# Hybrid decoder layer: softmax scaling, mix residuals and sums of squares go from GpSimd to VectorE

## The chip, the cores and the metric

The kernel runs on one core of one Trainium2 chip. The metric is device time in microseconds (us); lower is better. The engines are named as in the profile: PE is TensorE (matmuls; PEld its weight loads), DVE is VectorE, ACT is ScalarE, POOL is GpSimd, SP is SyncE, which issues the DMAs. [...]

## The reference

One layer over 1024 tokens of width 1024, in float32:

```python
h = rms_norm(x, norm_mix_g)
q, k, v, u, gate = split(h @ w_in)             # 512, 128, 128, 512, 512 columns
q = rms_norm(q per head, q_norm_g); k = rms_norm(k per head, k_norm_g)
a = sliding_window_gqa(q, k, v, sinks, rel_bias)   # 8 query heads, 2 kv heads, window 128
c = conformer_conv(u, gate, ...)                   # GLU, causal depthwise conv, layer norm, silu
mix = concat([rms_norm(a, attn_out_g), rms_norm(c, conv_out_g)])
x = x + mix @ w_out
h = rms_norm(x, norm_mlp_g)
x = x + square(relu(h @ w_mlp_up)) @ w_mlp_down    # hidden 4096
```

Inside the attention, for each block of 128 queries against the 256 keys of the block before and its own:

```python
s = q k^T * scale + bias, masked
m = max(max(s), sink)
p = exp(s - m)
p = p / (sum(p) + exp(sink - m))
o = p v
```

## The kernel before, in words

Tokens lie on the free axis, in two halves of 512 (`h` = 0 and 1), and channels on the partitions, in tiles of 128x512. Each float32 operand of the large products is split in two rounded parts, `hi` and `lo`, and a product is three matmuls (`whi` by `hi`, `whi` by `lo`, `wlo` by `hi`): L198 to L200 in the projections, L837 to L839 in the MLP's first part. The splits of the weights are L167 (`whi`, ACT) and L168 (`wlo`, DVE).

After the input projection the work is a list of generators that a hand-written string interleaves (input projection, attention units, convolution groups, norms, output projection, MLP). A tile framework then sets the order on each engine by a simulated time line, with raised priorities for some of the steps, so that an edit in one place can move instructions on every engine. PSUM has two banks for `mm` (products), two for `sc` (scores and broadcasts), two for `tr` (transposes), one for `o` and one for `x`. A product can begin only when an `mm` bank has been read out.

The attention is 16 units (head pair `j`, block pair `bp`), each in three steps that lie two units apart:
- `attn_a`: score matmuls (L567) into two `sc` banks, scaling by ACT (L574), then bias and row maximum by DVE (L575).
- `attn_b`: exponentials with their row sums by ACT (L591), the reciprocal `rd` of the sum by DVE (L594), and the scaling of the 128x1024 tile `s` by `rd` on POOL (L596, L597, L599). For the first block pair the tile is smaller, and this takes two instructions.
- `attn_c`: transposes of `s` (L616), their evacuation to `pT` (L603, on ACT or DVE by a table), the products with `v` (L625) into the `o` bank, and their evacuation into `Q` (L603).

`norm_half` normalises one half of one group (attention or conv) over its 512 channels. ACT squares each of the four sources (L637), DVE adds the squares into `nacc` (L638), PE sums over the partitions with four small matmuls (L642), DVE and POOL make the power −1/2 (L209, L210), PE broadcasts it (L393), DVE scales the four tiles (L648), ACT rounds each to the `hi` part of `mix` (L658), and POOL subtracts for the `lo` part (L659).

`out_conv` forms the conv half of the output projection: 12 matmuls into one `mm` bank, and DVE adds `x` to it (L727, tiles `X`, `Xp`, `Xq`). `out` does the attention half: 12 matmuls, DVE adds (L738), ACT squares (L743), and POOL adds the squares into `rbc` (L744), from which `x1_norm` makes the scale of the MLP's norm. `xn` (L768) applies that norm, and L763 (ACT) and L764 (DVE) split its result `n` into `x1g` for the MLP. Between the norms and the projections of one half stand units, products or MLP pieces of the other, which PE does meanwhile.

POOL does nothing else but the powers and a few memsets. No DMA is issued from it.

Of the kernel before, what the change touches and what calls it, by code (L numbers as in the profile page):

```python
# [12 lines left out]
F32 = mybir.dt.float32  # L13
F32R = mybir.dt.float32r
AF = mybir.ActivationFunctionType
ALU = mybir.AluOpType
AX = mybir.AxisListType

P = 128
# [48 lines left out]
class Builder:  # L68
# [42 lines left out]
    def dma(self, out, in_):  # L111
        d = self.nc.sync.dma_start(out, in_)
        if self.pinned:
            self.tc.keep_in_program_order(d)
        return d.ins
# [90 lines left out]
    def rsqrt(self, out, in_, scale, cols):  # L206
        nc = self.nc
        t = self.small("rs", cols)
        nc.vector.tensor_scalar(t, in_, scale, EPS, ALU.mult, ALU.add)  # L209
        nc.gpsimd.tensor_tensor(out, t, self.mhalf[:, :cols], ALU.pow)  # L210
# [368 lines left out]
    def attn_b(self, u):  # L579
        nc = self.nc  # L580
        s, j, bp = u["s"], u["j"], u["bp"]
        ns = self.nsink[:, j].rearrange("p b g -> p (b g)")
        nm, es, den, rd = (self.small(x, 4) for x in ("nm", "es", "den", "rd"))
        nc.vector.scalar_tensor_tensor(nm, u["mx"], -1.0, ns, ALU.mult, ALU.min)
        nc.vector.tensor_tensor(es, nm, ns, ALU.subtract)
        for i in range(4):
            lo = P if bp == 0 and i < 2 else 0
            with ExitStack() as c:
                if self.exp_after is not None:
                    c.enter_context(self.tc.issue_after(self.exp_after))  # L590
                nc.scalar.activation(s[:, i, lo:], s[:, i, lo:], AF.Exp, bias=nm[:, i:i + 1], accum_out=den[:, i:i + 1])  # L591
        self.last_exp = nc.scalar.activation(es, es, AF.Exp).ins
        nc.vector.tensor_tensor(den, den, es, ALU.add)
        nc.vector.reciprocal(rd, den)  # L594
        if bp == 0:
            nc.gpsimd.tensor_tensor(s[:, 0:2, P:], s[:, 0:2, P:], rd[:, 0:2].unsqueeze(2).broadcast_to([P, 2, P]), ALU.mult)  # L596
            nc.gpsimd.tensor_tensor(s[:, 2:4, :], s[:, 2:4, :], rd[:, 2:4].unsqueeze(2).broadcast_to([P, 2, 256]), ALU.mult)  # L597
        else:
            nc.gpsimd.tensor_tensor(s, s, rd.unsqueeze(2).broadcast_to([P, 4, 256]), ALU.mult)  # L599

    def evac(self, e, dst, src):
        nc = self.nc
# [26 lines left out]
    def norm_half(self, h, srcs, goff, kc0):  # L629
        nc = self.nc  # L630
        acc = self.half("nacc")
        for j, s in enumerate(srcs):
            if j == 0:
                nc.scalar.square(acc, s)
            else:
                sq = self.half("sq")
                nc.scalar.square(sq, s)  # L637
                nc.vector.tensor_tensor(acc, acc, sq, ALU.add)  # L638
        yield True
        ps = self.psum(TAGS["ns"])  # L640
        for i in range(4):
            nc.tensor.matmul(ps[:, i:i + 1], acc[:, i * P:(i + 1) * P], self.ones[:, 0:1], start=True, stop=True)  # L642
        rc = self.small("rc", 4)
        self.rsqrt(rc, ps[:, 0:4], 1.0 / 512, 4)
        yield True
        rb = self.bcast_ps(rc, TAGS["nb"])
        for j, s in enumerate(srcs):
            nc.vector.scalar_tensor_tensor(s, s, self.pv[:, goff + j:goff + j + 1], rb, ALU.mult, ALU.mult)  # L648
            if kc0 == 0:
                mt = self.a4(F32R, "mix", (P, 2, HT))  # L650
            elif h == 0:
                mt = self.mp.tile([P, 2, HT], F32R, tag="hg", name=self.nm("mix"), bufs=4)
            else:
                if j % 2 == 0:
                    pair = self.sp.tile([P, 2, 2, HT], F32R, tag="tw", name=self.nm("mix"), bufs=2)
                mt = pair[:, j % 2]
            self.mix[kc0 + j, h] = (mt[:, 0, :], mt[:, 1, :])
            nc.scalar.copy(mt[:, 0, :], s)  # L658
            nc.gpsimd.tensor_tensor(mt[:, 1, :], s, mt[:, 0, :].bitcast(F32), ALU.subtract)  # L659
        yield True  # L660

    def norm_attn(self, h):
# [67 lines left out]
    def out(self, h):  # L730
        nc = self.nc
        acc = self.rbc[:, self.hs(h)]
        for m in range(KC):
            w = self.next_w()
            ps = self.psum("mm")
            self.mm3(ps, w, [self.mix[kc, h] for kc in range(4)])
            X = self.X[m, h]
            nc.vector.tensor_tensor(X, ps, X, ALU.add)  # L738
            if m == 0:
                nc.scalar.square(acc, X)  # L740
            else:
                sq = self.half("sq")
                nc.scalar.square(sq, X)  # L743
                nc.gpsimd.tensor_tensor(acc, acc, sq, ALU.add)  # L744
            if m == KC - 1:
                self.sumsq[h] = acc
            yield True
# [409 lines left out]
```

## Time and profile before

| what | value |
|---|---|
| time before, median of 3 runs | 1023.99 us (1022.13 to 1025.24) |
| profiled execution: its own time / its span | 1022.33 us / 1020.4 us |
| mean granted TensorE clock | 0.983 |
| PE busy | 996.5 us, 98% of the span |
| DVE busy | 668.7 us, 66% |
| ACT busy | 493.2 us, 48% |
| POOL busy | 104.1 us, 10%, 82 instructions |

The profiled execution is one of the program's runs, and its span lies 1.93 us under its own time. Busy shares are means over the whole span. The input projection, the attention with the convolution, the output projection and the MLP follow one another with some overlap; the attention units lie at about 190 to 340 us after the span's start, and from about 420 us on only the MLP is left. POOL is busy between about 130 and 415 us only.

### The profile page before, as it was taken

The numbers are of one execution on the slowest core, as the hardware profiler recorded it, in microseconds if no ns is written. First come the engines' busy times: TensorE is split into PE (matmuls) and PEld (weight loads), VectorE is DVE, ScalarE is ACT, GpSimd is POOL, SyncE is SP. The second block draws the span as 40 slices with busy tenths as digits, with TensorE's granted clock in tenths as the row PEclk, the third lists the DMA queues.
The fourth block names the chain that finished last, engine by engine and source line by source line (L and its number), as shares of the span: only waits on it lengthen the run. The fifth ranks groups of instructions, "written<-read, shape, count | busy, mean of one in ns | idle before, by whom it ended". The sixth has DMA issues, their size and how long they took to land.

```text
span 1020.4 us, 14870 instructions
## 1 busy us (share of the span) xinstructions
PE 996.5 (98%) x5560; PEld 806.2 (79%) x5560; DVE 668.7 (66%) x1150; ACT 493.2 (48%) x946; POOL 104.1 (10%) x82
## 2 busy tenths in 40 slices
PE   8999999899979989999999999999999999999998
PEld 7888887677657768778888888888888888888886
DVE  7456535266667484598777786777774777747763
ACT  7332325766757445475444544536454343443442
POOL 1000012255143322200000000000000000000000
PEclk9999999799979999999999999999999999999999
DMA  9123300002200234446556655667875532346451
GB/s 354 60 70 136 125 32 11 11 12 93 73 11 32 90 122 139 145 171 215 194 194 220 237 185 205 239 225 255 285 264 188 183 130 99 103 135 216 165 165 42
DMA packets 67464, 148.72 MB, mean 146 GB/s; under 512 B 7776, under 2 KB 8032, under 8 KB 66880
## 3 DMA queue, kind: packets, MB, share of 16 engines
q1 hardware_dynamic: 67248, 147.75, 42.3%
q8 instruction: 44, 0.72, 0.3%
q14 instruction: 28, 0.23, 0.1%
q10 hardware_dynamic: 144, 0.02, 0.0%
HBM read 106.98 MB, written 38.80 MB: 143 GB/s over the span
## 4 chain that ended last, share of the span: by engine, by line
PE 89%; DVE 5%; ACT 3%; issue 1%; DMA 1%; POOL 0%; DVEq 0%; SPq 0%; ACTq 0%
PE mm L198 7%; PE mm L199 7%; PE mm L200 7%; PE sc L837 4%; PE sc L839 4%; PE sc L838 4%; PE tr L839 3%; PE tr L837 3%; PE tr L838 3%; PE sc L567 3%; PE mm L839 3%; PE mm L837 3%; PE mm L838 3%; PE mm L1057 3%; PE mm L1058 3%; PE mm L1059 3%
## 5 line engine op out<-in xcount | busy, mean ns | idle before, releaser
L763 ACT CAST wb<-wd 128x512 fp32r<-128x512 f32 x80 | 49.8, 622 | 111.3 <-DVE wd L1025 41.7
L764 DVE TENSOR_TENSOR wb<-wd,wb 128x512 fp32r<-128x512 f32 x80 | 55.3, 691 | 69.9 <-ACT wb L763 69.9
L167 ACT CAST whi<-raw 128x512 fp32r<-128x512 f32 (+1 forms) x54 | 42.9, 795 | 77.2 <-PE mm L199 55.4
L198 PE MATMUL mm<-xh,whi 128*128 128x512 f32 x192 | 77.8, 405 | 0.0
L199 PE MATMUL mm<-xl,whi 128*128 128x512 f32 x192 | 77.2, 402 | 0.0
L200 PE MATMUL mm<-xh,wlo 128*128 128x512 f32 x192 | 77.2, 402 | 0.0
L764 DVE TENSOR_TENSOR wb<-hb,wb 128x512 fp32r<-128x512 f32 x112 | 76.8, 685 | 0.0
L837 PE MATMUL sc<-op,wb 128*128 128x512 f32 x192 | 74.7, 389 | 0.0
L838 PE MATMUL sc<-op,wb 128*128 128x512 f32 x192 | 74.7, 389 | 0.0
L839 PE MATMUL sc<-op,wb 128*128 128x512 f32 x192 | 74.7, 389 | 0.0
L763 ACT CAST wb<-hb 128x512 fp32r<-128x512 f32 x112 | 69.0, 616 | 0.3 <-PE sc L839 0.3
L168 DVE TENSOR_TENSOR wlo<-raw,whi 128x512 fp32r<-128x512 f32 (+1 forms) x54 | 52.8, 979 | 16.8 <-ACT whi L167 11.5
L763 ACT CAST wb<-raw 128x512 fp32r<-128x512 f32 x46 | 27.7, 621 | 65.4 <-DVE raw L891 33.0
L198 PE MATMUL mm<-mix,whi 128*128 128x512 f32 x128 | 52.6, 412 | 3.3 <-ACT x1g L763 2.9
L200 PE MATMUL mm<-mix,wlo 128*128 128x512 f32 x128 | 52.5, 410 | 0.3 <-DVE wlo L168 0.3
L199 PE MATMUL mm<-mix,whi 128*128 128x512 f32 x128 | 52.4, 410 | 0.0
L1058 PE MATMUL mm<-wb,wb 128*128 128x512 f32 x128 | 49.8, 389 | 0.0
L1058 PE MATMUL sc<-wb,wb 128*128 128x512 f32 x128 | 49.8, 389 | 0.0
L837 PE MATMUL tr<-op,wb 128*128 128x512 f32 x128 | 49.8, 389 | 0.0
L838 PE MATMUL tr<-op,wb 128*128 128x512 f32 x128 | 49.8, 389 | 0.0
L1059 PE MATMUL mm<-wb,wb 128*128 128x512 f32 x128 | 49.6, 389 | 0.0
L1059 PE MATMUL sc<-wb,wb 128*128 128x512 f32 x128 | 49.6, 389 | 0.0
(270 smaller groups left out, 2532.9 us busy)
## 6 DMA issues: line engine op xcount, KB each, us to landing
hb<-hid SPq DMA_DIRECT2D x112, 256.0 KB, 2.9
wd<-w_down SPq DMA_DIRECT2D x80, 256.0 KB, 4.4
raw<-w_up SPq DMA_DIRECT2D x27, 512.0 KB, 3.5
hid<-h SPq DMA_DIRECT2D x48, 256.0 KB, 2.9
pa<-pa SPq DMA_DIRECT2D x20, 512.0 KB, 4.5
raw<-w_out SPq DMA_DIRECT2D x32, 256.0 KB, 2.6
hid<-pa SPq DMA_DIRECT2D x32, 256.0 KB, 2.9
hid<-tu SPq DMA_DIRECT2D x32, 256.0 KB, 3.3
```

Of the source, the lines that this page charges most:

```text
L167: self.pin(nc.scalar.copy(hi, raw))
L168: self.pin(eng.tensor_tensor(lo, raw, hi.bitcast(F32), ALU.subtract))
L198: nc.tensor.matmul(ps, w[0][:, ws], xh, start=first, stop=False)
L199: nc.tensor.matmul(ps, w[0][:, ws], xl, start=False, stop=False)
L200: nc.tensor.matmul(ps, w[1][:, ws], xh, start=False, stop=last)
L763: self.pin(self.nc.scalar.copy(hi, src))
L764: self.pin(eng.tensor_tensor(lo, src, hi.bitcast(F32), ALU.subtract))
L837: nc.tensor.matmul(ps, wh[:, c], xh, start=first and k == 0, stop=False, skip_group_check=True)
L838: nc.tensor.matmul(ps, wh[:, c], xl, start=False, stop=False, skip_group_check=True)
L839: nc.tensor.matmul(ps, wl[:, c], xh, start=False, stop=last and k == len(xs) - 1, skip_group_check=True)
L1058: nc.tensor.matmul(pss[m], wh[:, c], bl, start=False, stop=False, skip_group_check=True)
L1059: nc.tensor.matmul(pss[m], wl[:, c], bh, start=False, stop=f == NP - 1, skip_group_check=True)
```

## The change

Three kinds of POOL instructions become DVE instructions; POOL keeps the powers (L210, L375, L507). The scaling of `s` was one instruction per unit (two for `bp` = 0), with `rd` broadcast over the row; it becomes four per unit, one for each row block, with `rd` as the scalar operand. That makes 56 of 128x256 and 8 of 128x128. The 16 subtractions of `mix` and the 14 additions into `rbc` only change their engine.

```diff
@@ attn_b
         nc.vector.reciprocal(rd, den)
-        if bp == 0:
-            nc.gpsimd.tensor_tensor(s[:, 0:2, P:], s[:, 0:2, P:], rd[:, 0:2].unsqueeze(2).broadcast_to([P, 2, P]), ALU.mult)
-            nc.gpsimd.tensor_tensor(s[:, 2:4, :], s[:, 2:4, :], rd[:, 2:4].unsqueeze(2).broadcast_to([P, 2, 256]), ALU.mult)
-        else:
-            nc.gpsimd.tensor_tensor(s, s, rd.unsqueeze(2).broadcast_to([P, 4, 256]), ALU.mult)
+        for i in range(4):
+            lo = P if bp == 0 and i < 2 else 0
+            nc.vector.tensor_scalar(s[:, i, lo:], s[:, i, lo:], rd[:, i:i + 1], None, ALU.mult)
@@ norm_half
             nc.scalar.copy(mt[:, 0, :], s)
-            nc.gpsimd.tensor_tensor(mt[:, 1, :], s, mt[:, 0, :].bitcast(F32), ALU.subtract)
+            nc.vector.tensor_tensor(mt[:, 1, :], s, mt[:, 0, :].bitcast(F32), ALU.subtract)
@@ out
                 nc.scalar.square(sq, X)
-                nc.gpsimd.tensor_tensor(acc, acc, sq, ALU.add)
+                nc.vector.tensor_tensor(acc, acc, sq, ALU.add)
```

Lines behind the first edit have a number lower by two in the changed kernel (L642 becomes L640, L648 L646, L727 L725), and the scaling is its L597.

The framework gives another order on the engines. Two places matter.

The first is PE around the sum over partitions of the first attention norm (L642 before, on `nacc_2748`; L640 after, on `nacc_2774`). Before, this stands in a row on PE, from the products with `v` (`o_2686`) that are the last to go into that sum to the broadcast of its power:

```order
L625 MATMUL o_2686<-pT_2687,v 64x128 x2
L567 MATMUL sc_2712<-kh,Q_501 128x256 x2
L625 MATMUL o_2686<-pT_2687,v 64x128 x6
L616 MATMUL tr_2811<-ident,s_2463 128x128 x4
L616 MATMUL tr_2879<-ident,s_2561 128x128 x4
L616 MATMUL tr_2885<-ident,s_2561 128x128 x4
L642 MATMUL o_2759<-ones,nacc_2748 128x1 x4
L625 MATMUL o_2803<-pT_2804,v 64x128 x8
L393 MATMUL sc_2768<-ident,rc_2764 128x128 x4
```

Now this does, where `o_2712` are the same products:

```order
L614 MATMUL tr_2834<-ident,s_2480 128x128
L623 MATMUL o_2712<-pT_2713,v 64x128 x8
L614 MATMUL tr_2834<-ident,s_2480 128x128 x3
L614 MATMUL tr_2840<-ident,s_2480 128x128 x4
L198 MATMUL mm_2759<-mix_1967,whi_2674 128x512
L199 MATMUL mm_2759<-mix_1967,whi_2674 128x512
L200 MATMUL mm_2759<-mix_1967,wlo_2675 128x512
L614 MATMUL tr_2911<-ident,s_2581 128x128 x4
L614 MATMUL tr_2917<-ident,s_2581 128x128 x4
L640 MATMUL o_2785<-ones,nacc_2774 128x1 x4
L623 MATMUL o_2832<-pT_2833,v 64x128 x8
L393 MATMUL sc_2794<-ident,rc_2790 128x128 x4
```

Matmuls of the conv half of the output projection (`mm_2759`) have moved in between; the 9 of `mm_2759` before these three, and the last 3 of `mm_2680`, stand directly ahead of the first row, where before the same matmuls (as `mm_2733` and `mm_2657`) all stood earlier, ahead of the scores and transposes that come before these rows.

The second is DVE around the scaling of the second attention norm (L648 before, L646 after), where the conv half of the output projection ends and the MLP's norm of the first half begins. Before, it does:

```order
L648 SCALAR_TENSOR_TENSOR Q_501<-Q_501,pv,sc_3383 128x512 x4
L768 SCALAR_TENSOR_TENSOR n_571_3404<-Xp_2329,pv,rbc 128x512
L768 SCALAR_TENSOR_TENSOR n_578_3431<-Xp_2329,pv,rbc 128x512
L727 TENSOR_TENSOR Xq_3339<-mm_3449,xr_3447 128x512
L168 TENSOR_TENSOR wlo_3475<-raw_3409,whi_3474 128x512
L727 TENSOR_TENSOR X_3493<-mm_3480,xr_3478 128x512
L768 SCALAR_TENSOR_TENSOR n_578_3431<-X_2598,pv,rbc 128x512
L168 TENSOR_TENSOR wlo_3506<-raw_3441,whi_3505 128x512
```

Now it does (`mm_3493`, `mm_3524` and `mm_3555` are the products that were `mm_3449`, `mm_3480` and `mm_3511`):

```order
L725 TENSOR_TENSOR Xq_3383<-mm_3493,xr_3491 128x512
L168 TENSOR_TENSOR wlo_3519<-raw_3453,whi_3518 128x512
L646 SCALAR_TENSOR_TENSOR Q_501<-Q_501,pv,sc_3427 128x512 x4
L725 TENSOR_TENSOR X_3537<-mm_3524,xr_3522 128x512
L657 TENSOR_TENSOR mix_3433<-Q_501,mix_3433 128x512
L168 TENSOR_TENSOR wlo_3550<-raw_3485,whi_3549 128x512
L657 TENSOR_TENSOR mix_3437<-Q_501,mix_3437 128x512
L657 TENSOR_TENSOR mix_3441<-Q_501,mix_3441 128x512
L657 TENSOR_TENSOR mix_3445<-Q_501,mix_3445 128x512
L766 SCALAR_TENSOR_TENSOR n_571_3448<-Xp_2341,pv,rbc 128x512
L766 SCALAR_TENSOR_TENSOR n_578_3475<-Xp_2341,pv,rbc 128x512
L766 SCALAR_TENSOR_TENSOR n_578_3475<-X_2618,pv,rbc 128x512
```

The evacuation of `mm_3493` has moved ahead of the four scalings, and the four subtractions L657, which were POOL's, stand with three `xn` ahead of the evacuation of `mm_3555`, which is the next row. Behind that row come a weight split, the evacuation of the following product (`mm_3582`), a weight split of 128x1024, the two `lo` parts `x1g_3450` and `x1g_3477`, three more `xn`, the evacuation of `mm_3605`, another weight split of 128x1024, and the `lo` part `x1g_3482`. On PE, 5 matmuls of `mm_3524` follow the broadcast `sc_3427`, then the 12 of `mm_3555`, the 12 of `mm_3582`, the 12 of `mm_3605`, and the MLP's `mm_3627` from `x1g_3450`, `x1g_3477`, `x1g_3482` and `x1g_3509`, three matmuls each.

## Rows read from the trace of the kernel before

**Rows 1.** The page: span, and busy time of each engine.

```profile
span 1020.4 us, 14870 instructions
PE 996.5 (98%) x5560; PEld 806.2 (79%) x5560; DVE 668.7 (66%) x1150; ACT 493.2 (48%) x946; POOL 104.1 (10%) x82
```

**Rows 2.** Windows: stretch, length, PE, PEld, DVE, ACT, POOL busy, PEclk, DMA share, GB/s.

```profile
320.00:350.00 30.00, 30.00 (x192) 22.41 (x193) 16.80 (x31) 18.70 (x44) 13.71 (x9) 1.00 0.19 62
350.00:380.00 30.00, 26.61 (x124) 21.45 (x123) 23.15 (x36) 12.11 (x21) 8.41 (x6) 0.94 0.38 124
600.00:700.00 100.00, 100.00 (x443) 82.77 (x442) 74.59 (x120) 46.47 (x82) 0.00 (x0) 1.00 0.66 231
```

**Rows 3.** Windows of two more stretches.

```profile
397.00:415.00 18.00, 18.00 (x81) 14.92 (x80) 9.00 (x12) 8.63 (x13) 9.72 (x7) 1.00 0.44 147
...
200.00:283.00 83.00, 83.00 (x460) 61.02 (x460) 51.99 (x149) 56.25 (x162) 34.54 (x23) 0.96 0.18 58
```

**Rows 4.** Windows around the two attention norms.

```profile
283.50:289.20 5.70, 1.46 (x13) 0.99 (x11) 3.42 (x13) 5.63 (x22) 1.89 (x1) 0.88 0.00 0
289.20:309.00 19.80, 18.43 (x77) 13.19 (x77) 11.37 (x25) 8.17 (x22) 10.13 (x7) 0.60 0.00 1
361.90:390.00 28.10, 24.71 (x101) 19.35 (x101) 23.23 (x32) 13.32 (x23) 6.41 (x4) 0.94 0.29 95
```

**Rows 5.** PE's time line, 280 to 298 us: start, us, instruction, [idle before].

```profile
286.59 0.66 PE L616 MATMUL tr<-ident,s 128*128 128x128 f32 x4 [2.29 <-ACT pT L603]
289.20 1.87 PE L642 MATMUL o<-ones,nacc 128*128 128x1 f32 x8 [1.95 <-DVE nacc L638]
```

**Rows 6.** POOL's time line, 276 to 302 us.

```profile
280.02 1.89 POOL L599 TENSOR_TENSOR s<-s,rd 128x1024 f32<-128x1024 f32 x1 [7.72 <-DVE rd L594]
286.70 1.89 POOL L599 TENSOR_TENSOR s<-s,rd 128x1024 f32<-128x1024 f32 x1 [4.79 <-DVE es L585]
```

**Rows 7.** DVE's time line, 276 to 288 us.

```profile
280.09 2.11 DVE L575 CUSTOM_DVE_ANT_0 s<-s,bias 128x256 f32<-128x256 f32 x1
...
285.74 0.43 DVE L575 CUSTOM_DVE_ANT_0 s<-s,bias 128x256 f32<-128x256 f32 x1
...
287.10 2.04 DVE L638 TENSOR_TENSOR nacc<-nacc,sq 128x512 f32<-128x512 f32 x1 [0.52 <-ACT sq L637]
```

**Rows 8.** The chain of waits, 276 to 300 us: start, us, what.

```profile
286.54 0.54 ACT sq L637
```

**Rows 9.** POOL's groups: count, busy us, mean ns, idle before and its releasers.

```profile
L599 POOL TENSOR_TENSOR s<-s,rd 128x1024 f32<-128x1024 f32 x12 | 23.8, 1980 | 49.2 <-DVE rd L594 17.8 <-ACT whi L167 9.9 <-PE o L625 8.9
L744 POOL TENSOR_TENSOR rbc<-rbc,sq 128x512 f32<-128x512 f32 x14 | 19.5, 1392 | 49.7 <-ACT sq L743 45.8 <-ACT es L592 4.0
...
L659 POOL TENSOR_TENSOR mix<-Q,mix 128x512 fp32r<-128x512 f32 x8 | 11.8, 1502 | 10.8 <-ACT mix L658 10.8
L659 POOL TENSOR_TENSOR mix<-y,mix 128x512 fp32r<-128x512 f32 x8 | 11.0, 1390 | 5.0 <-ACT mix L658 5.0
```

**Rows 10.** DVE's groups, shapes apart.

```profile
L764 DVE TENSOR_TENSOR wb<-hb,wb 128x512 fp32r<-128x512 f32 x112 | 76.8, 685 | 0.0
L575 DVE CUSTOM_DVE_ANT_0 s<-s,bias 128x256 f32<-128x256 f32 x56 | 37.8, 706 | 6.0 <-ACT s L574 5.8
...
L603 DVE COPY Q<-o 128x256 f32<-128x256 f32 x6 | 2.5, 424 | 5.1 <-PE o L625 5.1
...
L518 DVE COPY kc<-rk 128x512 f32<-128x512 f32 x2 | 0.8, 424 | 0.0
```

**Rows 11.** The time line of all engines, 361.9 to 369 us.

```profile
362.26 2.72 DVE L648 SCALAR_TENSOR_TENSOR Q<-Q,pv,sc 128x512 f32<-128x512 f32 x4 [2.99 <-PE sc L393]
...
364.90 2.42 DVE L768 SCALAR_TENSOR_TENSOR n<-Xp,pv,rbc 128x512 f32<-128x512 f32 x2
...
367.24 0.68 DVE L727 TENSOR_TENSOR Xq<-mm,xr 128x512 f32<-128x512 f32 x1
...
368.07 0.47 PE L198 MATMUL mm<-mix,whi 128*128 128x512 f32 x1 [2.87 <-ACT x1g L763]
```

## The prediction

> **What bounds the kernel now.** I read the page first. PE is busy for 996.5 of 1020.4 us [rows 1], so anything this change can win is time in which PE waits, or runs at the lower clock level. The windows say where that is. From 420 us on nothing that the change touches is left, and there PE is full: 100.00 busy of 100.00 us, clock 1.00, 443 matmuls, so 0.2257 us for one of 128x512 [rows 2]. From 200 to 283 us PE is full as well (83.00 of 83.00), although most of the units are scaled there and half of the `mix` subtractions done; so it is from 320 to 350 us [rows 2, 3]. PE waits in two places, each at an attention norm [rows 4]: 4.24 us from 283.5 to 289.2 and another 1.37 us up to 309, and 3.39 us from 361.9 to 390. Behind the first wait the granted clock falls: 0.60 on average over 19.80 us. With only the levels 1.0 and 0.5, that is the lower one for 80% of it, 15.8 us, which cost at most 7.9 us.
>
> The time lines then show why PE waits. At 286.59 it had waited 2.29 us for transposes, and at 289.20 1.95 us for the sum of squares `nacc` [rows 5]. Both go back to a DVE instruction that was slow beside a POOL one: the bias step begun at 280.09 took 2.11 us while POOL scaled `s` from 280.02 for 1.89; the same step at 285.74, beside no POOL work, took 0.43. The add into `nacc`, begun at 287.10, took 2.04 beside the next scaling (286.70, 1.89) [rows 6, 7], where an add of this shape has a mean of 0.685 [rows 10]. So in these places the two engines did not work side by side: the DVE instruction ended when POOL's did.
>
> The second place is another story. PE waited 2.87 us at 368.07; the row names an ACT split, but that matmul begins a new product, and what came free last for it is the `mm` bank, read out by the DVE add begun at 367.24. This add stood behind the four scalings of `Q` (362.26, 2.72 us) and two `xn` (364.90, 2.42 us) [rows 11].
>
> **The change part by part.** *What DVE takes on.* The nearest rows for a scaling of 128x256 are 0.43 (the bias step, two inputs and a maximum [rows 7]) from above and half of the 0.424 of a 128x512 copy between SBUF tiles, 0.21, from below; a 128x256 copy out of PSUM took 0.424 [rows 10]. I take 0.35, and 0.30 for the eight halves: 56 x 0.35 + 8 x 0.30 = 22.0 us. The 16 subtractions are the shape and kind of L764, 0.685 each, 11.0 us; the 14 adds likewise, 9.6 us. Together 42.6 us. What DVE gets back is the stretch under POOL: the 56 bias steps alone took 37.8 us and at 0.43 would take 24.1, so at least 13.7 us; at most what POOL spent in the four groups that go, 66.1 us [rows 9, 10]. I take 25, about twice the one group. DVE ends near 686 us, 67% of the span: not a bound as a whole, but each of its queues counts.
>
> *A. First attention norm, 283 to 309 us.* The chain that ends in `nacc` is now: evacuation of `o` 0.42 [rows 10], the square 0.54 [rows 8], the add 0.685, with gaps some 2 us. PE has in that time, by the new order, 15 transposes (four took 0.66 [rows 5], so 2.5 us if none overlap) and three matmuls of 0.23: 3.2 us. So the sum need not wait. The wait of 2.29 us for transposes falls for two reasons: the bias step is no longer stretched, which gives 1.68 us, and 12 matmuls (2.7 us) now stand ahead of them. I leave 0.7 us of the 4.24 for what is late next (the broadcast's chain through POOL's power, which stays): −3.5, bounds 0 and −4.24. The clock: it fell behind a gap of 5.70 us in which PE did 1.46 us of work [rows 4]. If that gap is filled, the fall may not come, −7.9; the rest of the norm's chain (sum, power, broadcast, scaling, split) is still there with little PE work beside it, so it may come as before, 0. No row tells which; I take less than half, −3.5. A = −7.0, bounds 0 and −12.1.
>
> [...]
>
> *B. Second attention norm, 362 to 390 us.* Now: 28.10 us for 101 matmuls, which at 0.2257 want 22.8, so 5.3 us lost: 3.39 of waiting and, at a clock of 0.94, 1.7 by the lower level [rows 2, 4]. After: the evacuation of `mm_3493` is moved ahead of the scalings, so the wait of 2.87 goes. Take its successor, `mm_3555`, in time from the broadcast `sc_3427`. DVE does four scalings (2.72), one add, four subtractions, a split and three `xn`, then the add that frees the bank: ten more of 0.62 (the mean in the full stretch, 74.59 us for 120 [rows 2]) to 0.685, so 8.9 to 9.6 us. PE has 5 + 12 + 12 matmuls until it needs that bank, 29 x 0.2257 = 6.5 us, and 0.3 to 0.5 us more as the split in that queue is late for it. It waits 2.0 to 2.5 us. Then the MLP's first product: its `lo` part `x1g_3482` is 11 DVE instructions further on, two of them of double length, so 13 x 0.62 to 0.685 = 8.1 to 8.9 us after the bank. PE has 12 + 7 matmuls for that time, 4.3 us, and loses 3.8 to 4.6 us, part of it already at the `hi` parts. With the 0.3 to 0.5 for the split and some 0.5 at the product after, 6.6 to 8.1 us are lost in place of 5.3, if the clock holds; one more spell at the lower level adds 1.7. I take 7.5: B = +2.2, bounds 0 (DVE faster than 0.62 with POOL silent) and +4.6.
>
> *C. The other units, and the `mix` subtractions of the convolution, 191 to 283 and 302 to 350 us.* PE is full there [rows 2, 3], which is what hides POOL's work now and DVE's then; DVE is busy 63% and 56% of it. 0; bounds −3.3 (clock 0.96 over 83 us, if it stayed up) and +2 (one more spell at the lower level).
>
> *D. The sums of squares, seven in 320 to 350 and seven in 397 to 415 us.* They end in a norm that is wanted much later. In 397 to 415 us PE is full and DVE half idle (9.00 of 18.00); seven adds of 0.685 fill 4.8 us of the 9.0 [rows 3]. 0; without that cover they would cost their 4.8 us.
>
> Sum: −7.0 + 2.2 = −4.8 us. The profiled execution goes from 1022.33 to 1017.5 us; it lies 1.66 us under the median of the runs, so for that 1023.99 − 4.8 = **1019.2 us**.
>
> **The rivals.** *Nothing to measure.* The first norm gains little (−2 to −3: the waits shrink, the clock falls all the same), and the second takes it back (+2.2): 1023 to 1024. For it speaks that PE was full in most of the stretch; against it that 4.24 us of waiting has its cause in the stretched instructions.
>
> *Both clock terms fall away:* A is −12.1 and B as above, −9.9: 1014. For it: the fall came behind a gap that should close.
>
> *Slower by DVE's queue at the second norm.* The bank of `mm_3555` comes free behind four subtractions that POOL had done beside DVE. If 8.1 us are lost, the clock falls once more (B = +4.6), and at the first norm only 1.4 us is won: +3.2, 1027.2. It decides itself where that bank comes free later than 6.5 us after the broadcast; by the order it does, so the question is the size.
>
> *Slower by small pieces.* One unit is now scaled in four instructions, 1.4 us of DVE's queue per unit where POOL's 1.98 stood beside it. If the evacuations and the splits of weights behind them come 0.7 us late (half of it) for PE in each of the 11 units between 200 and 302 us, that is +7.7, with −4.8 together +2.9: 1026.9. Against it: PE is full in 83.00 us of 83.00 with DVE at 51.99 even with all the stretch.
>
> [...]
>
> **How the numbers follow.** About 0.3%, 3.1 us, is what a measurement of this kernel can tell from no change. Forecast (A −5 to −9, B +1 to +3) 0.42; both clock terms gone 0.18; nothing to measure 0.20; DVE's queue 0.13; small pieces 0.07. So faster 0.60, same 0.20, slower 0.20. The forecast's own range is 1016 to 1022 us. For 8 in 10 the range goes down to 1010.5 (the best case with some of C's bound) and up to 1027.5 (the slower cases).
>
> **What would show it.** Right: POOL about 30 us; no bias step above 0.5 us except beside a power; no PE wait above 1 us between 283 and 290 us; a wait of about 2 us at the first matmul of `mm_3605` and of 3 us or more at a `lo` part of `x1g`; windows from 420 us on unchanged. A clock of 0.6 behind the first norm would take half of A away. Wrong: PE waits in 200 to 283 us, behind DVE's scalings or evacuations; or scalings of 0.5 us and more each, since B's and C's queues then are longer than I worked out.

## The result, and the profile after

The changed kernel takes 1011.66 us (median of 4 runs, 1009.68 to 1013.01), the one before 1023.12 us beside it: a ratio of 0.9882, with a 95% interval of 0.9864 to 0.9901, so 11.5 us less. It was forecast at 1019.2. The profiled execution went from a span of 1020.4 to 1010.1 us.

The page of the changed kernel, to be held against [rows 1]:

```profile
span 1010.1 us, 14850 instructions
...
PE 989.2 (98%) x5560; PEld 802.9 (79%) x5560; DVE 677.4 (67%) x1244; ACT 491.8 (49%) x946; POOL 30.9 (3%) x32
```

Its windows (columns as in [rows 2]); the stretches answer to those of [rows 2 to 4]:

```profile
200.00:283.00 83.00, 83.00 (x450) 62.19 (x451) 52.07 (x194) 58.01 (x171) 10.08 (x4) 0.95 0.15 50
283.50:289.20 5.70, 5.45 (x53) 4.42 (x50) 4.79 (x16) 4.40 (x14) 1.01 (x1) 1.00 0.30 94
289.20:309.00 19.80, 18.87 (x117) 13.34 (x118) 16.82 (x59) 14.26 (x41) 0.00 (x0) 1.00 0.04 14
...
350.00:380.00 30.00, 24.81 (x101) 18.43 (x100) 22.89 (x35) 13.13 (x22) 0.00 (x0) 0.94 0.27 90
...
600.00:700.00 100.00, 100.00 (x443) 82.84 (x442) 72.93 (x118) 47.60 (x83) 0.00 (x0) 1.00 0.67 233
```

At the first attention norm PE is now busy for 5.45 of 5.70 us where it was for 1.46, and in the 19.80 us behind it the clock is 1.00 where it was 0.60. The second norm still has its waits, and from 420 us on nothing moved.

DVE's groups, shapes apart:

```profile
L575 DVE CUSTOM_DVE_ANT_0 s<-s,bias 128x256 f32<-128x256 f32 x56 | 22.4, 420 | 5.1 <-ACT s L574 4.8
...
L597 DVE TENSOR_SCALAR s<-s,rd 128x256 f32<-128x256 f32 x56 | 16.2, 349 | 0.3
...
L742 DVE TENSOR_TENSOR rbc<-rbc,sq 128x512 f32<-128x512 f32 x14 | 9.7, 690 | 0.8
...
L657 DVE TENSOR_TENSOR mix<-Q,mix 128x512 fp32r<-128x512 f32 x8 | 5.2, 686 | 0.0
...
L597 DVE TENSOR_SCALAR s<-s,rd 128x128 f32<-128x128 f32 x8 | 1.9, 282 | 0.1
```

The bias step went from a mean of 706 ns [rows 10] to 420: no instruction stands beside a scaling on POOL any more. PE's time line at the first norm, where [rows 5] had two waits of about 2 us:

```profile
286.44 1.04 PE L640 MATMUL o<-ones,nacc 128*128 128x1 f32 x8
287.73 1.09 PE L623 MATMUL o<-pT,v 128*64 128x128 f32 x16 [0.26 <-DVE rs L209]
...
291.96 1.13 PE L567 MATMUL sc<-kh,Q 64*128 64x256 f32 x4 [0.93 <-ACT s L574]
```

And at the second norm, 340 to 395 us, the two longest waits:

```profile
360.58 0.47 PE L198 MATMUL mm<-mix,whi 128*128 128x512 f32 x1 [1.91 <-ACT x1g L761]
...
368.35 0.50 PE L836 MATMUL mm<-x1g,whi 128*128 128x512 f32 x1 [2.50 <-DVE x1g L762]
```

DVE's time line ahead of the first of them shows the queue that was forecast:

```profile
351.51 2.72 DVE L646 SCALAR_TENSOR_TENSOR Q<-Q,pv,sc 128x512 f32<-128x512 f32 x4 [1.20 <-PE sc L393]
354.15 0.68 DVE L725 TENSOR_TENSOR X<-mm,xr 128x512 f32<-128x512 f32 x1
354.75 0.68 DVE L657 TENSOR_TENSOR mix<-Q,mix 128x512 fp32r<-128x512 f32 x1
...
355.95 1.89 DVE L657 TENSOR_TENSOR mix<-Q,mix 128x512 fp32r<-128x512 f32 x3
357.76 1.41 DVE L766 SCALAR_TENSOR_TENSOR n<-Xp,pv,rbc 128x512 f32<-128x512 f32 x2
...
359.75 0.69 DVE L725 TENSOR_TENSOR X<-mm,xr 128x512 f32<-128x512 f32 x1
```

The add at 359.75 frees the bank, and PE's matmul at 360.58 is the one that needed it.

**A ledger.** Two numbers of each profile explain most of what sets its span apart from the others': PE's idle time (the span less PE's busy time) and what the lower clock level costs. In windows of 0.1 us of the kernel before, the granted clock is 1.00 or 0.50 in 10,190 of 10,200; sixteen matmuls of L625 took 1.10 us at 1.00 (begun at 270.44) and 1.98 at 0.50 (begun at 305.74). With these two levels, the cost is at most (1 − mean clock) x span. The clock has three digits, so this is good to about 0.5 us. Rows of kernels from the experiments below are put in already.

| kernel | span | PE busy | idle | clock | lost by clock | rest |
|---|---|---|---|---|---|---|
| before | 1020.4 | 996.5 | 23.9 | 0.983 | 17.3 | 979.2 |
| full change | 1010.1 | 989.2 | 20.9 | 0.990 | 10.1 | 979.1 |
| scaling alone | 1019.2 | 997.0 | 22.2 | 0.982 | 18.3 | 978.7 |
| residuals of the mix alone | 1016.1 | 995.0 | 21.1 | 0.985 | 15.2 | 979.8 |
| full change, POOL loaded | 1016.3 | 994.2 | 22.1 | 0.985 | 15.2 | 979.0 |
| before, empty work on PE | 1016.5 | 995.8 | 20.7 | 0.991 | 9.1 | 986.7 |
| full change, subtractions later | 1004.6 | 985.3 | 19.3 | 0.993 | 7.0 | 978.3 |

The rest of these is the same within 1.5 us but for the kernel that has work added on PE; the seven profiles that are not in the table come to 977.8 to 980.6. So of the change's 10.3 us, 3.0 are PE's waits and 7.2 the clock, as far as this sum tells them apart.

### The profile page after: what moved, and what is told of

It reads as the page before. It is cut to its first block, busy times and chain, and to the rows that moved or that the text cites. A ratio compares the mean times of both kernels' runs of the same rounds, so it can differ in the third digit from the quotient of the medians.

```text
span 1010.1 us, 14850 instructions
## 1 busy us (share of the span) xinstructions
PE 989.2 (98%) x5560; PEld 802.9 (79%) x5560; DVE 677.4 (67%) x1244; ACT 491.8 (49%) x946; POOL 30.9 (3%) x32
## 3 DMA queue, kind: packets, MB, share of 16 engines
q1 hardware_dynamic: 67248, 147.75, 42.6%
## 4 chain that ended last, share of the span: by engine, by line
PE 90%; DVE 5%; ACT 3%; DMA 1%; issue 1%; SPq 0%; POOL 0%; DVEq 0%; ACTq 0%
PE mm L198 7%; PE mm L199 7%; PE mm L200 7%; PE sc L837 4%; PE sc L835 4%; PE sc L836 4%; PE tr L837 3%; PE tr L835 3%; PE tr L836 3%; PE sc L567 3%; PE mm L1055 3%; PE mm L1056 3%; PE mm L1057 3%; PE sc L1057 3%; PE sc L1055 3%; PE sc L1056 3%
## 5 line engine op out<-in xcount | busy, mean ns | idle before, releaser
L168 DVE TENSOR_TENSOR wlo<-raw,whi 128x512 fp32r<-128x512 f32 (+1 forms) x54 | 48.6, 901 | 17.4 <-ACT whi L167 12.3
L198 PE MATMUL mm<-mix,whi 128*128 128x512 f32 x128 | 51.2, 401 | 1.9 <-ACT x1g L761 1.9
L199 PE MATMUL mm<-mix,whi 128*128 128x512 f32 x128 | 50.6, 396 | 0.0
```

Of the source, the lines that this page charges most:

```text
L168: self.pin(eng.tensor_tensor(lo, raw, hi.bitcast(F32), ALU.subtract))
L198: nc.tensor.matmul(ps, w[0][:, ws], xh, start=first, stop=False)
L199: nc.tensor.matmul(ps, w[0][:, ws], xl, start=False, stop=False)
```

## The experiments

All ratios are to the kernel before, run beside on the same chip, with their 95% interval.

**One part at a time.** Three kernels each take one part of the diff:

```diff
 e1:  for i in range(4): nc.vector.tensor_scalar(s[:, i, lo:], ...)       # scaling only
 e2:  nc.vector.tensor_tensor(mt[:, 1, :], s, mt[:, 0, :] ..., subtract)   # residuals of the mix only
 e3:  nc.vector.tensor_tensor(acc, acc, sq, ALU.add)                       # sums of squares only
```

The scaling alone:

> Only the softmax scaling goes to VectorE; the residuals of the mix and the sums of squares stay on GpSimd. Theory P (the gain is the stretched VectorE work at the first attention norm, which the scalings on GpSimd cause): nearly the whole gain of the first norm is here, 8 to 11 us, and the second norm costs no more than before, since the four subtractions are still on GpSimd: 1011 to 1015 us, at or a little below the full change. Theory Q (all three parts add up, each by freeing its own stretched time): 3 to 6 us less than before, 1017 to 1020 us.

1020.78 us, 0.996 (0.994 to 0.998): theory P's time fell. The windows of this kernel say why:

```profile
225.00:250.00 25.00, 25.00 (x105) 17.88 (x102) 12.70 (x47) 14.77 (x44) 5.48 (x4) 0.65 0.06 22
...
283.00:309.00 26.00, 24.77 (x162) 17.62 (x162) 20.49 (x58) 16.89 (x49) 6.54 (x5) 1.00 0.20 62
```

The first norm was won, with 1.2 us of waiting and a clock of 1.00. But from 225 to 250 us, at the second convolution norm, the clock is 0.65, where before and after it is 0.93, and that takes most of the gain back. PE shows no idle time there. Its order at that place has changed: scores, the small sums, transposes and the broadcast follow one another with only a few large matmuls between. So what theory P said of the first norm holds, and the loss lies elsewhere.

The residuals alone:

> Only the 16 residuals of the mix go to VectorE. TensorE's order is that of before, row for row. Theory P: the first norm's waits of 2.29 and 1.95 us stay (the scalings still stand beside the bias step and the add), and the second norm gets the longer VectorE queue: 0 to +4 us against before. Theory Q: 2 to 4 us less than before.

1019.06 us, 0.9947 (0.9927 to 0.9967): 5.0 us less, a little beyond theory Q's figure and against P's. PE's order is that of before, but the scalings on POOL now fall at other moments. PE's time line, 270 to 312 us, and the windows at the norm:

```profile
284.91 0.66 PE L616 MATMUL tr<-ident,s 128*128 128x128 f32 x4 [0.70 <-ACT pT L603]
...
287.02 1.05 PE L642 MATMUL o<-ones,nacc 128*128 128x1 f32 x8 [1.45 <-DVE nacc L638]
```

```profile
283.50:289.20 5.70, 3.29 (x35) 2.71 (x33) 3.93 (x16) 3.50 (x12) 0.92 (x2) 1.00 0.30 92
289.20:309.00 19.80, 19.80 (x77) 13.49 (x73) 10.74 (x32) 9.64 (x27) 2.01 (x2) 0.66 0.00 1
```

The two waits of [rows 5] shrank from 4.24 to 2.15 us, since the add into `nacc` is no longer the instruction that is caught (0.68 us at 286.28 for 2.04). But the clock behind is 0.66, hardly above the 0.60 of before: with half of the wait gone, most of the spell at the lower level stays.

The sums alone:

> Only the 14 additions of squares go to VectorE. TensorE's order is that of before. Both theories of the stages say 0 (-1 to +1 us): TensorE is full where they lie. If GpSimd work anywhere costs time, -2 to -4 us.

1023.8 us, 1.0001 (0.9984 to 1.0017): nothing, as forecast. Their counterpart is the full change without them:

> The full change with the 14 sums of squares back on GpSimd. TensorE's order is that of the full change but for 9 rows. The sums alone did nothing, so the time should be that of the full change, 1010.5 to 1013 us; if the sums matter once the rest is gone, 1013 to 1016 us.

1012.85 us, 0.989 (0.9876 to 0.9905): the full change's time.

**Which residuals the scaling lacks.** The scaling and the convolution's residuals only:

```diff
+ (nc.vector if kc0 else nc.gpsimd).tensor_tensor(mt[:, 1, :], s, mt[:, 0, :]..., subtract)   # on e1
```

> The scaling and the eight residuals of the convolution's mix on VectorE; the eight of the attention and the sums of squares stay on GpSimd. The scaling alone had won the first attention norm, but lost most of it again to a spell of 20.5 us at the lower level from 232.5 us on, at the second convolution norm, where its order has few large matmuls; in this kernel the order at that place is that of the full change. Theory R (the convolution's residuals on GpSimd push that place into the bad order): the spell there is 3.4 us as in the full change, and the time 1010 to 1014 us. If the attention's residuals or the sums are what the scaling lacked: 1018 to 1021 us as with the scaling alone.

1009.63 us, 0.9862 (0.9843 to 0.9881): theory R by the time, just under its range. Its window at the second convolution norm:

```profile
225.00:250.00 25.00, 25.00 (x132) 18.59 (x130) 15.04 (x51) 15.85 (x44) 3.91 (x2) 0.86 0.19 53
```

The clock is 0.86 here, against 0.65 with the scaling alone. But the spell is about 7 us long, not the 3.4 that theory R named: the full change has 0.93, with PE's order at that place the same. So that order is not all that sets the spell. These two parts are the whole gain of the change; the sums and the attention's residuals add nothing to it.

**Order or stretch.** The full change moves instructions and frees DVE from POOL at once. This kernel keeps the order of the full change and loads POOL again:

```diff
+ for i in range(3):
+     nc.gpsimd.tensor_tensor(scr, scr, rd[:, i:i + 1].broadcast_to([P, 256]), ALU.mult)
```

> The full change, and behind each reciprocal three two-input GpSimd instructions of 128x256 on a tile that nothing else uses (0.66 us each by the rows of before, 32 us in all and some). The orders of VectorE and ScalarE are those of the full change, TensorE's too but for 8 rows. Theory S (stretch: work on GpSimd that reads SBUF holds VectorE up): bias steps of 2 us come back, VectorE's busy time grows by 10 to 25 us, and time grows by 2 to 8 us: 1014 to 1020 us. Theory O (the new order, with matmuls of the output projection at the first norm, is what won the time): no more than 1.5 us over the full change, 1011 to 1013.5 us, even with stretched instructions.

1016.7 us, 0.9925 (0.9907 to 0.9942): some 5 us over the full change, in theory S's range, but 6.8 us are still won against before. Its sign was another one, though: the bias steps stayed at 416 ns on average, and the scalings were stretched. A unit on DVE's and on POOL's time line:

```profile
273.78 2.36 DVE L599 TENSOR_SCALAR s<-s,rd 128x256 f32<-128x256 f32 x4
```

```profile
273.88 2.10 POOL L601 TENSOR_TENSOR scr<-scr,rd 128x256 f32<-128x256 f32 x3 [5.07 <-DVE rd L596]
```

DVE's group and the windows at the first norm:

```profile
L599 DVE TENSOR_SCALAR s<-s,rd 128x256 f32<-128x256 f32 x56 | 32.6, 638 | 0.3
```

```profile
283.50:289.20 5.70, 3.91 (x35) 2.70 (x33) 4.58 (x16) 3.42 (x12) 1.64 (x2) 1.00 0.30 92
289.20:309.00 19.80, 18.87 (x72) 13.12 (x73) 13.66 (x40) 10.44 (x33) 2.16 (x4) 0.66 0.05 14
```

The four scalings, beside POOL's three, now take 638 ns each for 349, and DVE's busy time grew by 17 us. On PE, whose order at the norm is that of the full change, two waits are new:

```profile
285.55 0.66 PE L618 MATMUL tr<-ident,s 128*128 128x128 f32 x4 [0.99 <-DVE pT L605]
...
289.16 1.64 PE L395 MATMUL sc<-ident,rc 128*128 128x128 f32 x8 [0.53 <-POOL rc L210]
```

With them the clock behind the norm is 0.66 again. So the stretch brings the lower level back even in the new order, and the full change needed the freed DVE. What the new order is worth by itself is not shown: no run has the old order with DVE freed.

The control with instructions on POOL that read nothing:

> Control of the run before: the same places, but GpSimd only sets the tile (8 instructions of 128x256 that read nothing, about 2 us in all per unit). If any GpSimd work holds VectorE up, the same 2 to 8 us over the full change; if it takes GpSimd instructions that read SBUF, bias steps stay at 0.42 us and the time within 1 us of the full change.

1014.12 us, 0.9893 (0.987 to 0.9916). It settles nothing: nothing held the memsets to the reciprocals, and they ran from 3 to 56 us, far from the attention. With a release that holds them there:

```diff
+ nc.vector.tensor_copy(scr[:, 0:1], rd[:, 0:1])
+ for _ in range(7):                             # behind the scalings
+     nc.gpsimd.memset(scr, 0.0)
```

> The control again, since in the first one the memsets ran from 3 to 56 us, far from the attention: a VectorE copy of one column behind each reciprocal now releases seven GpSimd memsets of 128x256 (0.31 us each by the first control, 2.2 us per unit), so that they lie beside the scalings. The order changes in about 100 of VectorE's 1200 rows, so the time tells little (1009 to 1019 us). The durations tell: if GpSimd work that reads nothing holds VectorE up too, scalings of 0.6 us and more as with the two-input load (638 ns on average there); if it takes reading, 350 ns as in the full change.

1018.1 us, 0.9948 (0.9924 to 0.9973), with another order, so that the time alone tells nothing of the memsets. DVE's time line, and POOL's beside it:

```profile
270.03 1.53 DVE L600 TENSOR_SCALAR s<-s,rd 128x256 f32<-128x256 f32 x4
271.49 0.67 DVE L168 TENSOR_TENSOR wlo<-raw,whi 128x512 fp32r<-128x512 f32 x1
272.08 0.41 DVE L577 CUSTOM_DVE_ANT_0 s<-s,bias 128x256 f32<-128x256 f32 x1
```

```profile
270.18 2.75 POOL L602 MEMSET scr<- 128x256 f32 x7 [3.16 <-DVE scr L597]
```

Neither of the two answers: the scalings are held a little (four in 1.53 us against 1.14 in the full change, 423 ns on average against 349), while the split and the bias step behind them, beside the same memsets, take 0.67 and 0.41 us, as in the first control with no memset beside them (0.68 and 0.42).

**Clock or waits.** The kernel before, with empty work for PE at the first norm:

```diff
+ with self.tc.issue_after(self.last_po):         # the last products with v
+     for _ in range(10):
+         nc.tensor.matmul(fl, m[:, :P], m, start=True, stop=True)
+ for _ in range(2):
+     nc.tensor.matmul(fl, self.ident, sq, start=True, stop=True)
```

> The kernel before with empty work on TensorE in the two gaps at the first attention norm: 10 matmuls of 128x512 after the last products with v, and 2 float32 matmuls on the last square ahead of the sum; their bank is never read. Up to that place the orders are those of before, and the stretched instructions on VectorE stay. Theory C (the clock fell because TensorE did little in those gaps): the two spells of 6.83 and 10.24 us at the lower level go, 8.5 us less: 1014 to 1017 us, although no wait of another engine is shorter. If the clock falls from what follows the norm (power, broadcast), or if it is the waits themselves that cost: within 2 us of before, 1021 to 1025 us.

1019.12 us, 0.9953 (0.9938 to 0.9968). PE's time line, and the window behind:

```profile
283.74 2.12 PE L643 MATMUL x<-mix 128*128 128x512 f32 x8
...
287.31 1.98 PE L645 MATMUL x<-sq,ident 128*128 128x512 f32 x4
289.82 1.02 PE L649 MATMUL o<-ones,nacc 128*128 128x1 f32 x8 [0.53 <-DVE nacc L638]
```

```profile
289.20:309.00 19.80, 18.83 (x123) 13.18 (x123) 15.01 (x39) 11.07 (x35) 10.48 (x7) 1.00 0.00 1
```

Theory C is right on the mechanism: with POOL's scalings still there, work that is thrown away kept the clock at 1.00 for these 19.8 us, and the kernel was faster by it. It missed on the size: 4 us in place of 8.5. By the ledger 8.2 us came back from the clock and 3.2 from the waits, but the rest is 7.5 us larger; the empty work is 4 to 4.5 of that, and the other 3 are open (the order behind the norm differs).

**One large scaling or four small.**

```diff
- for i in range(4): nc.vector.tensor_scalar(s[:, i, lo:], ...)
+ nc.vector.tensor_tensor(s, s, rd.unsqueeze(2).broadcast_to([P, 4, 256]), ALU.mult)
```

> The full change, but each unit is scaled by one VectorE instruction (128x1024, rd broadcast over the row; two for the first block pair) in place of four small ones. Rival of the small pieces: one large instruction takes less of VectorE's time than four at 0.35 us each and wins 2 us or more: 1007 to 1010 us. If the small pieces cost nothing, within 2 us of the full change, 1010 to 1013 us; it is a two-input form, so that one may take as long as 1.1 to 1.3 us, no less than the four.

1014.25 us, 0.9905 (0.9884 to 0.9925), not faster than the full change:

```profile
L599 DVE TENSOR_TENSOR s<-s,rd 128x1024 f32<-128x1024 f32 x12 | 14.7, 1222 | 0.2
```

One takes 1.22 us; four small ones follow one another at 16.2 / 56 = 0.29 us, 1.16 in all.

**The second norm.** The four subtractions of that norm are taken out of DVE's queue, first behind the first add of the MLP, then behind the last `x1g`:

```diff
- nc.vector.tensor_tensor(mt[:, 1, :], s, mt[:, 0, :]..., subtract)       # for kc0 == 0, h == 1
+ with self.tc.issue_after(self.pa_ins):     # e4; e8: self.x1_ins, the last residual of x1g
+     for mt, s in self.late: nc.vector.tensor_tensor(mt[:, 1, :], s, mt[:, 0, :]..., subtract)
```

> The full change, but the four subtractions of the second attention norm are put behind the first addition of the MLP's first part, where VectorE waits for TensorE. Theory of the queue (the wait at the second norm is VectorE's queue ahead of the bank's evacuation): the wait of 1.91 us for the bank goes, that of 2.50 us for the residual of the MLP input shrinks to about 2, and the spell at the lower clock (1.7 us) may go too: 2 to 4 us less than the full change, 1007.5 to 1009.5 us. If these waits are not VectorE's queue but the products of the norm or ScalarE, no change, 1011 to 1012 us.

1012.2 us, 0.989 (0.9865 to 0.9914). Both waits went, and the time did not. DVE's and PE's time lines:

```profile
374.41 2.49 DVE L667 TENSOR_TENSOR mix<-Q,mix 128x512 fp32r<-128x512 f32 x4
376.81 0.68 DVE L865 TENSOR_TENSOR pa<-pa,mm 128x512 f32<-128x512 f32 x1
```

```profile
377.64 0.47 PE L199 MATMUL mm<-mix,whi 128*128 128x512 f32 x1 [1.99 <-DVE pa L865]
```

The same four instructions now stand ahead of another evacuation. Hence the second place, where DVE had 4.29 us to spare in that run:

> The full change with the four subtractions of the second attention norm behind the last residual of the MLP input, where VectorE waits 4.29 us for TensorE. In the run with the subtractions still later both waits of the second norm had gone, but two new ones of 0.42 and 1.99 us had come for a bank that VectorE read out behind the subtractions. Queue theory: these go as well, and with them the last 3.4 us spell at the lower level: 3 to 5 us under the full change, 1007 to 1009 us. If the second norm only hands its wait on to the next place, 1011 to 1012 us again.

1006.44 us, 0.9823 (0.9803 to 0.9843). The window from 350 to 392 us, of the kernel before, of the full change and of this kernel:

```profile
350.00:392.00 42.00, 38.61 (x177) 31.36 (x176) 29.93 (x45) 18.64 (x31) 8.41 (x6) 0.96 0.36 118
```

```profile
350.00:392.00 42.00, 36.81 (x154) 28.37 (x153) 30.53 (x47) 19.58 (x32) 0.00 (x0) 0.96 0.35 119
```

```profile
350.00:392.00 42.00, 38.79 (x166) 30.08 (x165) 33.51 (x52) 21.56 (x36) 0.00 (x0) 1.00 0.41 134
```

This kernel beats both: 17 us less than before and some 5 less than the full change.

## Why the prediction was right, and where its size was off

The direction held, and so did the wide range, 1010.5 to 1027.5; the forecast's own range, 1016 to 1022, did not. The likeliest number was 7.5 us too high, and the time came out nearest the rival that had 0.18, "both clock terms fall away" (1014).

- **What bounds it**: right. 600 to 700 us is the same row to the digit in PE, and all of the difference lies before 420 us.
- **What DVE takes on**: 0.35 us were taken for a scaling, 349 ns measured; 0.30 for the halves, 282 ns; 0.685 for the others, 686 and 690. In busy time they are 38.1 us and not 42.6, since small ones follow one another at 0.29. The stretch given back is 668.7 + 38.1 − 677.4 = 29.4 us; 25 were taken. (The upper bound, 66.1 us of POOL's time, left out the scalings of the first block pair; POOL lost 104.1 − 30.9 = 73.2.)
- **A, the waits**: −3.5 taken, −4.4 measured (4.24 + 1.37 before, 0.25 + 0.93 after). The sum no longer waits, as worked out. One reading was loose: the two slow DVE instructions ended 0.29 and 0.55 us after POOL's, not with it.
- **A, the clock**: this step failed in size. "I take less than half, −3.5": the whole of it went. In the two windows it cost 7.9 and 0.7 us before, nothing after. The empty work on PE shows that the gap ahead of the sum was what brought the lower level on (a clock of 1.00 over the 19.80 us behind it, for 0.60), so with the gap filled there was no reason to keep half of it. Nor did the clock come back in step with the gap: with the residuals alone PE waited for 2.41 of the 5.70 us and with POOL loaded for 1.79, and behind both it was 0.66. Of the two causes that I named for the gap, the freed DVE is shown, since loading POOL again in the new order cost some 5 of the 11.5 us; the share of the 12 matmuls that moved is not.
- **B**: the sum came out, in part by luck. +2.2 taken; from 350 to 392 us PE waits 5.19 us where it waited 3.39, +1.8, at the same clock of 0.96. I had put 6.6 to 8.1 us of waiting and no spell at the lower level; the waits were shorter, and a spell stayed that cost 1.7 us. The bank cost 1.91 us (2.0 to 2.5 worked out), the `lo` part 2.50 with 0.5 at the `hi` parts (3.8 to 4.6): DVE's subtractions, adds and splits followed at 0.60 us and the `xn` at 0.66, so about 0.62 on average, the lower price. The runs with the subtractions moved show the queue as the cause.
- **C**: 0 as a sum, and 0.9 us lost in the rest of the span. But "PE is full there, which hides it" was too short: full does not mean at full clock. In this stretch the scaling alone lost most of what it won, without a microsecond of idle time (clock 0.65 from 225 to 250 us).
- **D**: right, 1.0001.
- **Small pieces**: fell. From start to start one takes 0.29 us, so a unit 1.16 where 1.4 was worked out. Half the elements still take 282 ns for 349, so part of the time does not go with the size, but the one large form has two inputs and is no faster (1.22 us for 1.16).

## What to carry to other kernels

Where two engines hold each other up (2.11 us for 0.43 here), look for the one place where that stands on the path; the sum over the kernel (29.4 us of stretch here) says little about it. Then price the clock with the wait: a gap of a few microseconds on TensorE cost more behind itself (7.9 us) than in itself (4.2). The change that closed it won all of that, and the two runs that only shortened it won little of it (a clock of 0.66 behind it, for 0.60). After moving work to an engine that does it faster (four scalings in 1.16 us on VectorE for 1.98 on GpSimd), look at what now stands ahead of each PSUM evacuation in its queue, and put what is not urgent where that engine waits anyway (some 5 us here).

## What the runs showed of the hardware that I had not expected

**The clock fell without idle time.** With the scaling alone, PE is busy for 25.00 of 25.00 us, as the profile counts it, at a clock of 0.65. And runs of one kernel differ in the clock: with the scaling alone, those at a mean of 0.987 took 1016.5 us, those at 0.982 about 1021. Only one of them has a trace, so what sets them apart is open.

**Not all work on GpSimd held VectorE up.** Two-input arithmetic did (the bias step took 2.11 us for 0.43, [rows 6, 7], and a scaling 638 ns for 349 with POOL loaded). Memsets held the scalings a little (423 ns for 349) and the split and the bias step behind them not at all (0.67 and 0.41 us). Two powers held neither the scalings nor the bias step; POOL's and DVE's time lines of the full change:

```profile
232.90 1.01 POOL L210 TENSOR_TENSOR rc<-rs,mhalf 128x4 f32<-128x4 f32 x1 [8.94 <-DVE den L593]
235.69 2.90 POOL L507 TENSOR_TENSOR qst<-qst,mhalf 128x16 f32<-128x16 f32 x1 [1.78 <-DVE qst L506]
```

```profile
233.34 1.00 DVE L597 TENSOR_SCALAR s<-s,rd 128x128 f32<-128x128 f32 x4
...
236.29 0.42 DVE L575 CUSTOM_DVE_ANT_0 s<-s,bias 128x256 f32<-128x256 f32 x1 [0.75 <-ACT s L574]
```

Four scalings of 128x128 took 1.00 us, begun beside a power, where four beside none took 1.01 at 194 us, and the bias step ran through at 0.42 us in the middle of a power of 2.90 us. What tells the memsets and the powers from the rest is not shown; and the power's 2.90 us hold only as far as the profile has its span right.
